# The output product of a hybrid decoder block: eight products of quarters or seven

## The chip, the cores and the metric

The kernel runs on one core of a Trainium2 chip. The core has five engines that run side by side, each with its own queue of instructions: TensorE (PE; its weight loads are shown as PEld), VectorE (DVE), ScalarE (ACT), GpSimd (POOL) and SyncE (SP), which here only starts transfers. The metric is the device time of one execution in microseconds (us), the median of several runs.

## The reference, cut to what matters

The model is one pre-norm decoder layer: 512 tokens, width 1024. Three branches read the normalized input; their gated sum goes through `w_o`, is added to `x`, and a gated convolutional feed-forward block and a last norm follow.

```
u      = rmsnorm(x, ln1_g)
proj   = u @ w_in                      # q, k, v, pool, z, xbc, dt, gates
merged = g0 * (attention @ w_a) + g1 * (pooling @ w_b) + g2 * (ssd @ w_c)
x      = x + merged @ w_o              # the output product: 512 x 1024 by 1024 x 1024
u2     = rmsnorm(x, ln2_g)
x      = x + conv_ffn(u2 @ w_up, ...) @ w_down
out    = rmsnorm(x, final_g)
```

All is float32. TensorE multiplies in fp32r, so every product is made from three: high part by high part, high by low, low by high, where the high part is the value cast to fp32r and the low part what the cast left over (`mm3`, L228).

## The kernel before, in words

**Jobs.** The work is a list of jobs (`program`, L1491). Each job multiplies one piece of weights, usually 128 x 2048 elements: 1 MB that SP loads into `raw` (two buffers), ACT casts to the high part `wh` (two casts of half the columns, L195), and DVE subtracts to the low part `wl` (L215). The loop at L1715 runs the list: as job n begins, `prepare` (L1723) writes the low part of job n+1, then the cast of job n+2, then starts the load of job n+3; then the job's own matmuls are written. A job may have a `form`, a function that makes its weights just ahead of the cast, and a `then`, called behind its low part. With `late` the job's body calls `prepare` itself.

**Order.** PE, ACT, DVE and POOL have their order written out: the program's order is the queue's order (`ORDERED`, L1748). SP's transfers are placed by the scheduler. Work beside the matmuls is in generators: `step()` (L155) moves every generator in `running` on by one yield; `after(n, it)` (L163) holds one back for n steps. So a step is the clock by which side work is laid between matmuls.

**w_c, the third branch.** `branch_jobs(2, w_c, ..., last=True)` (L1219) makes the eight 128-feature pieces m = 0 to 7 of the merged branches, two per job, 24 matmuls of 512 columns each. Its `evac` multiplies by the gate (L1226), adds to the sum `MG[m]` of the other branches (L1227) and splits the result into `MH[m]`, high and low (L1230, L1231). There is one step per piece.

**w_o, the output product.** `load_x1` (L1242) loads the norm's weights and eight 128 x 512 blocks of `x`, `X1[tb, h]`: row block tb (128 tokens), column half h. `wo_jobs(pair, h)` (L1249) computes two row blocks (pair 0: tb 0 and 1; pair 1: tb 2 and 3) of one column half in two jobs of 24 matmuls, four of the eight k slices in each: eight jobs in all, with one step per job. `evac` adds the PSUM bank to `X1` (L1252). After the left half, `norm_early` (L457) squares it on ACT, makes `v0` on DVE and `xg`, x times the norm's weight, on POOL (L462). After the right half, `norm_late` (L466) squares it on ACT, takes the root (L471), multiplies by the weight (L473), makes the factor with three small DVE instructions (L488 to L490) and scales both halves (L492). `norm_turn` (L447) then transposes the block on PE (L451), ACT copies the high part (L454) and DVE makes the low part (L455): `uh` and `ul`, the feed-forward's input. For pair 0 the transposes are held back by one step, for pair 1 they go into the opening of the up projection.

**The opening** (`opening`, L1410): the first two up jobs (up0, up1) multiply tokens 0 to 255 first (L1421), with the transposes of blocks 2 and 3 laid between; the rest of the up projection follows as ordinary matmuls "pu" at L236.

**Seven products.** Elsewhere the kernel already multiplies by quarters with seven products for eight: `Seven` (L344) for parts of w_in and `down_group` (L1349). `sums_of` (L321) makes the sums and differences of a pair of feature pieces: four half additions (L326 to L329), two casts, two low parts (L335, L336). `Seven` makes one weight sum by an adding transfer: `plus` (L354), four POOL transfers of 128 x 512 that add memory to a tile (L356); other weight sums are DVE's (`total`, L358). Tiles "w3" come from a pool of three buffers (`ypool`), shared with the state-space branch.

Of the kernel before, what the change touches and what calls it, by code (L numbers as in the profile page):

```python
# [10 lines left out]
F32 = mybir.dt.float32  # L11
F32R = mybir.dt.float32r
AF = mybir.ActivationFunctionType
OP = mybir.AluOpType
# [68 lines left out]
def trunk(ctx: ExitStack, tc, out, x, rel_bias, ln1_g, w_in, b_gate, w_a, pool_w, pool_scale, w_b,  # L83
# [22 lines left out]
    def T(name, dt=F32, shape=(P, S)):  # L106
        return big.tile(list(shape), dt, name=name, tag="t")
# [55 lines left out]
    def after(n, it):  # L163
        for _ in range(n):
            yield
        yield from it
# [58 lines left out]
    def wsrc(w, k0, k1, c0, c1):  # L225
        return w[k0 * P:k1 * P, c0:c1].rearrange("(k p) c -> p k c", p=P)
# [239 lines left out]
    def norm_late(t, g, v0, outs, last=None):  # L466
# [4 lines left out]
        act.activation(sq, ss, AF.Sqrt, bias=v0, scale=1.0 / D)  # L471
        xg = T("xg")
        dve.tensor_tensor(xg, t, g[1], OP.mult)  # L473
        if last:
            dve.scalar_tensor_tensor(v, ss, -0.5 / D, last, OP.mult, OP.add)
            yield xg

            dve.reciprocal(r, sq)
            dve.scalar_tensor_tensor(rt, r, v, r, OP.mult, OP.mult)
            dve.scalar_tensor_tensor(rt, rt, 1.5, r, OP.add, OP.mult)  # L480

            (o1, x1), (o0, x0) = outs(xg)
            act.mul(o0, x0, rt)
            dve.tensor_scalar(o1, x1, rt, None, OP.mult)
            return
        dve.scalar_tensor_tensor(v, ss, 1.0 / D, v0, OP.mult, OP.add)
        yield xg
        dve.reciprocal(r, sq)  # L488
        dve.scalar_tensor_tensor(rt, r, v, r, OP.mult, OP.mult)
        dve.tensor_scalar(rt, rt, -0.5, 1.5, OP.mult, OP.add)  # L490
        for o, src in outs(xg):
            dve.tensor_scalar(o, src, r, rt, OP.mult, OP.mult)  # L492

    V0 = []

# [708 lines left out]
                    dve.tensor_sub(YT[q][1], Y[gi][:, q % 4, :], YT[q][0].bitcast(F32))  # L1204


    MG, MH, SG = {}, {}, {}

    def gate_jobs(b, lo=0, hi=8):
        def evac(m, ps):  # L1210
# [5 lines left out]

        return jobs_a(w_in, C_GATE + b * D + lo * P, hi - lo, uhk, ulk, KD, evac)

    def branch_jobs(b, w, parts, nk, last=False, more=()):  # L1219
        def evac(m, ps):  # L1220
            if b == 1:
                MG[m] = T("yo")
                act.copy(MG[m], ps)
                return
            s = SG[b, m]
            dve.tensor_tensor(s, s, ps, OP.mult)  # L1226
            (dve if last else pool).tensor_tensor(MG[m], MG[m], s, OP.add)  # L1227
            if last:
                h, l = T("mgh", F32R), T("mgl", F32R)
                act.copy(h, MG[m])  # L1230
                dve.tensor_sub(l, MG[m], h.bitcast(F32))  # L1231
                MH[m] = (h, l)
# [8 lines left out]

    def load_x1():  # L1242
        nxt["g2"] = grow(ln2_g[0])
        for tb in range(4):
            for h in range(2):
                t = X1[tb, h] = T("x1")
                sp.dma_start(t, x[tb * P:(tb + 1) * P, h * S:(h + 1) * S])

    def wo_jobs(pair, h):  # L1249
        def evac(tb, ps):  # L1250
            t = X1[tb, h]
            dve.tensor_tensor(t, t, ps, OP.add)  # L1252
            if h == 0:
                nxt[tb] = norm_early(t, nxt["g2"])
                return
# [3 lines left out]
            v0, xg0 = nxt[tb]  # L1259
            us = [T("u0"), T("u1")]  # L1260
            it = norm_late(t, nxt["g2"], v0, lambda xg1: ((us[0], xg0), (us[1], xg1)))
# [20 lines left out]
        return jobs_b(lambda k0, k1: [wsrc(w_o, k0, k1, h * S, h * S + S)], S,  # L1282
                      lambda k, tb: MH[k][0][:, tb * P:(tb + 1) * P],
                      lambda k, tb: MH[k][1][:, tb * P:(tb + 1) * P], KD, evac,
                      blocks=(2 * pair, 2 * pair + 1), turn_over=pair == 1 and h == 1)


    ACTS = {}
    ff = {}
# [177 lines left out]
    def down_jobs(h):  # L1467

        def evac(tb, ps):
            t = X1[tb, h]  # L1470
            dve.tensor_tensor(t, t, ps, OP.add)
            if h == 0:
                running.append(early(tb))
                return
            v0, vh, xg0 = fin[tb]
            for _ in norm_late(t, fin["g"], v0, lambda xg1: ((xg1, xg1), (xg0, xg0)), last=vh):
# [14 lines left out]
    def program():  # L1491
# [49 lines left out]
        yield from branch_jobs(2, w_c, YT, 8, last=True)  # L1541
        yield Call(load_x1)
        for pair in range(2):
            for h in range(2):
                yield from wo_jobs(pair, h)
            if pair == 0:
# [237 lines left out]
```

## Time and profile before

| | |
|---|---|
| median of three runs | 1021.44 us (1021.38 to 1021.48) |
| the profiled execution: its time | 1021.86 us |
| its span, first to last instruction | 1019.9 us |
| PE busy | 1010.3 us (99%) |
| DVE busy | 707.4 us (69%) |
| ACT busy | 511.3 us (50%) |
| POOL busy | 136.4 us (13%) |
| granted PE clock | 0.998 |

In the rows of the profile, the first number of a timeline row is its start in us from the span's start, the second its length; then the engine, the line of the kernel, the operation, the tiles it writes and reads, their shape, and how many instructions are in the row. In square brackets stands how long the engine was idle before it, and behind the arrow what ended that. Tiles go by the program's names: `pb` are the banks of the output product, `pa` those of w_c and others, `pu` the up projection, `uT` the transposes, `raw`, `wh`, `wl` the weights, `mgh` and `mgl` the merged branches, `w` (for "w3") a weight sum.

### The profile page before, as it was taken

What the parts mean: (1) busy time and instruction counts of PE and PEld (TensorE: products, weight loads), DVE (VectorE), ACT (ScalarE), POOL (GpSimd) and SP (SyncE); (2) the same over time, 40 slices, a digit from 0 to 9 for tenths busy, and PEclk for the clock granted to TensorE, in tenths of its full rate; (3) what the DMA queues carried; (4) which work ended last, traced back from release to release, by engine and by line L of the source; (5) the groups of instructions that cost most, each with busy time, mean ns of one, the idle gap of its engine ahead of it and who ended that gap; (6) DMA issues with size and microseconds to landing.
All of it is one profiled execution on the core that took longest, in us unless ns stands there. A gap on an engine that the chain in (4) does not pass through costs nothing.

```text
span 1019.9 us, 13619 instructions
## 1 busy us (share of the span) xinstructions
PE 1010.3 (99%) x5402; PEld 862.2 (85%) x5402; DVE 707.4 (69%) x886; ACT 511.3 (50%) x863; POOL 136.4 (13%) x120
## 2 busy tenths in 40 slices
PE   8999999999999999999999999999999999999997
PEld 8998878999988888888888888898888888888885
DVE  6564768577767647666889665768778768685756
ACT  5433546564435476879467224554444444433434
POOL 1691000010000000000052501102111100111002
PEclk9999999999999999999999999999999999999999
DMA  8548222255254344552253427532332322321332
GB/s 270 170 101 210 92 74 76 58 149 162 91 183 113 91 124 104 145 141 87 81 155 127 165 85 272 163 124 83 105 102 83 106 101 83 123 83 42 124 103 82
DMA packets 115629, 123.34 MB, mean 121 GB/s; under 512 B 6483, under 2 KB 96150, under 8 KB 115567
## 3 DMA queue, kind: packets, MB, share of 16 engines
q1 hardware_dynamic: 113247, 119.01, 37.5%
q0 software_dynamic: 1728, 2.62, 1.5%
q8 instruction: 42, 0.69, 0.3%
q10 hardware_dynamic: 592, 0.86, 0.2%
q14 instruction: 20, 0.16, 0.0%
HBM read 118.68 MB, written 3.00 MB: 119 GB/s over the span
## 4 chain that ended last, share of the span: by engine, by line
PE 98%; DMA 1%; DVE 0%; ACT 0%; ACTq 0%; issue 0%
PE pa L236 36%; PE pu L236 22%; PE pb L236 12%; PE pd L236 7%; PE pqk L236 6%; PE pq L236 3%; PE pa L1632 2%; PE ps L786 1%; PE pu L1421 1%; PE ppw L236 1%; PE po L834 1%; PE pt L820 1%; PE py L1119 1%; DMA xin<-in_x_dram 1%; PE pyo L1126 1%; PE pst L1107 0%
## 5 line engine op out<-in xcount | busy, mean ns | idle before, releaser
L215 DVE TENSOR_TENSOR wl<-raw,wh 128x2048 fp32r<-128x2048 f32 (+3 forms) x92 | 214.1, 2328 | 51.5 <-ACT wh L195 38.8
L195 ACT CAST wh<-raw 128x1024 fp32r<-128x1024 f32 (+4 forms) x181 | 181.4, 1021 | 57.4 <-DVE raw L359 17.8
L1316 DVE SCALAR_TENSOR_TENSOR hc<-pu,fcol,hc 128x510 f32<-128x510 f32 x88 | 65.9, 748 | 56.2 <-ACT hc L1313 54.5
L236 PE MATMUL pa<-uh,wh 128*128 128x512 f32 (+1 forms) x368 | 88.8, 381 | 0.0
L236 PE MATMUL pa<-ul,wh 128*128 128x512 f32 (+1 forms) x368 | 86.8, 375 | 0.0
L236 PE MATMUL pa<-uh,wl 128*128 128x512 f32 (+1 forms) x368 | 86.8, 375 | 0.0
L236 PE MATMUL pu<-uh,wh 128*128 128x512 f32 (+1 forms) x352 | 83.5, 379 | 0.0
L236 PE MATMUL pu<-ul,wh 128*128 128x512 f32 (+1 forms) x352 | 83.5, 379 | 0.0
L236 PE MATMUL pu<-uh,wl 128*128 128x512 f32 (+1 forms) x352 | 83.5, 379 | 0.0
L236 PEld LDWEIGHTS pa<-ul,wh 128*128 128x128 f32 x368 | 66.7, 188 | 12.6
L236 PEld LDWEIGHTS pa<-uh,wl 128*128 128x128 f32 x368 | 66.7, 188 | 12.5
L236 PEld LDWEIGHTS pa<-uh,wh 128*128 128x128 f32 x368 | 65.4, 189 | 11.8
L236 PEld LDWEIGHTS pu<-ul,wh 128*128 128x128 f32 x352 | 64.2, 188 | 12.5
L236 PEld LDWEIGHTS pu<-uh,wl 128*128 128x128 f32 x352 | 64.2, 188 | 12.5
L236 PEld LDWEIGHTS pu<-uh,wh 128*128 128x128 f32 x352 | 64.1, 188 | 12.4
L1313 ACT ACTIVATE hc<-pu,fcol,fcol 128x512 f32<-128x512 f32 x40 | 31.2, 779 | 78.9 <-PE pu L236 78.9
L1321 POOL TENSOR_TENSOR hc<-hc 128x512 f32<-128x512 f32 x22 | 30.8, 1400 | 289.1 <-DVE hc L1316 244.4
L808 ACT ACTIVATE sb<-sb,nmls 128x128 f32<-128x128 f32 (+1 forms) x72 | 30.0, 418 | 31.4 <-DVE nmls L805 20.8
L215 DVE TENSOR_TENSOR wl<-w,wh 128x2048 fp32r<-128x2048 f32 (+1 forms) x18 | 38.0, 2111 | 10.2 <-issue 4.6
L1102 POOL TENSOR_TENSOR st<-st,dts 128x512 f32<-128x512 f32 x4 | 4.2, 1052 | 225.6 <-ACT st L1110 163.5
L195 ACT CAST wh<-w 128x1024 fp32r<-128x1024 f32 (+1 forms) x36 | 32.9, 954 | 2.4 <-DVE w L341 2.4
L1318 ACT ACTIVATE hc<-hc 128x512 f32<-128x512 f32 x22 | 13.9, 633 | 40.2 <-DVE hc L1316 40.2
(409 smaller groups left out, 1924.4 us busy)
## 6 DMA issues: line engine op xcount, KB each, us to landing
raw<-in_w_in_dram SPq DMA_DIRECT2D x24, 1024.0 KB, 5.8
raw<-in_ffn_w_up_dram SPq DMA_DIRECT2D x22, 1024.0 KB, 5.7
raw<-in_w_o_dram SPq DMA_DIRECT2D x8, 1024.0 KB, 5.1
raw<-in_ffn_w_down_dram SPq DMA_DIRECT2D x8, 1024.0 KB, 5.3
raw<-in_w_in_dram SPq DMA_DIRECT2D x14, 512.0 KB, 5.5
raw<-in_w_in_dram SPq DMA_DIRECT2D x8, 768.0 KB
raw<-in_w_b_dram SPq DMA_DIRECT2D x4, 1024.0 KB
w<-in_ffn_w_down_dram SPq DMA_DIRECT2D x4, 1024.0 KB, 5.0
```

Of the source, the lines that this page charges most:

```text
L195: (other.tensor_copy if other and i else act.copy)(job.high[:, :, o], job.raw[:, :, o])
L215: (eng or dve).tensor_tensor(l[:, :, o], job.raw[:, :, o], h[:, :, o].bitcast(F32), OP.subtract)
L236: pe.matmul(ps, l, r, start=first and n == 0, stop=last and n == total - 1, skip_group_check=onto)
L786: pe.matmul(pss[i][:, o:o + w * P], q[r, n * P:(n + 1) * P], k[r, kb * P:(kb + w) * P], start=True, stop=True)
L808: act.activation(sb[:, off:off + w * P], sb[:, off:off + w * P], AF.Exp, bias=nm[:, n, h:h + 1], accum_out=ls[:, n, h:h + 1])
L820: pe.transpose(pt[:, o:o + P], sb[:, o:o + P], eye)
L834: pe.matmul(po[DH * hh:DH * hh + DH, n * P:(n + 1) * P], V[g, kb + i][:, (2 * c + hh) * DH:(2 * c + hh + 1) * DH], probs[2 * c + hh, nb][: ...
L1313: act.activation(t, ps, AF.Identity, bias=ff["c1"][:, ff["b"] + m:ff["b"] + m + 1], scale=fw(2, m))
L1316: dve.scalar_tensor_tensor(t[:, sh:], ps[:, :S - sh], fw(k, m), t[:, sh:], OP.mult, OP.add)
L1318: act.activation(t, t, AF.Silu)
L1321: pool.tensor_tensor(a, a, t, OP.mult)
L1632: pe.matmul(first[2 * n + j][:, lo:hi], a[:, k, j * P:(j + 1) * P], b[:, k, lo:hi], start=a is wh and b is uh and k == 0, stop=a is wl and ...
```

## The change

The output product becomes one group of seven products of quarters. With the merged branches split by even and odd feature pieces and by token halves, and `w_o` by even and odd k slices and column halves, each of the seven jobs multiplies four k slices by 512 columns for two row blocks: 24 matmuls. Their order is two, five, three, one, six, seven, four.

- The job "two" needs the odd pieces' first token half, "four" the second, "one" the even pieces' first half; "five", "six", "seven" and "three" need the sums 1, 2, 3, 4 of `sums_of`. `merged(m)` makes these while w_c runs. For m = 4 and 5 the addition into `MG[m]` is an adding transfer, and `merged` starts a step later.
- Weights: W0 and W1 are loaded when w_c begins; W0 gets an adding transfer of another quarter at once (`plus(0, 0, 0)`), W1 a second one behind the low part of "three" (`three.then`); W2 = W0 + W1 on DVE, ahead of W1's addition, in w_c's third job. "five" uses W0, "three" the first W1, "six" W2, "seven" the second W1; "four" adds W2 to its raw weights (`total`, on DVE, ahead of its cast). Only "two", "one" and "four" load raw weights.
- Results: "two", "five" and "three" are copied from PSUM to `X1` by ACT, and `x` is added by a transfer, two each, six of the eight blocks. "one", "six", "seven" and "four" are added to or subtracted from `X1` by DVE.
- Bodies step after each row block's bank. "two" and "five" (`apart`) multiply three k slices of both row blocks, step, and then do the fourth.
- The norm: blocks 0 and 1 have their early half behind "one" and their late half behind "six", blocks 2 and 3 behind "seven" (right half first) and "four". The late form scales the late half with one DVE instruction (`apart` in `norm_late`) and the early half on ACT; the form with two DVE scalings goes.

The diff, cut to its core:

```diff
-    def norm_early(t, g):
+    def norm_early(t, g, h=0):
...
-        pool.tensor_tensor(xg, t, g[0], OP.mult)
+        pool.tensor_tensor(xg, t, g[h], OP.mult)
...
+    def norm_late(t, g, v0, outs, last, h=1, apart=False):
         ss, v, sq, r, rt = (small(n, [P, 1]) for n in ("ss", "v", "sq", "r", "rt"))
         squares(act, t, ss)
         act.activation(sq, ss, AF.Sqrt, bias=v0, scale=1.0 / D)
...
+        dve.scalar_tensor_tensor(v, ss, -0.5 / D, last, OP.mult, OP.add)
         yield xg
+
         dve.reciprocal(r, sq)
         dve.scalar_tensor_tensor(rt, r, v, r, OP.mult, OP.mult)
+        dve.scalar_tensor_tensor(rt, rt, 1.5, r, OP.add, OP.mult)
+
+        if apart:
+            o1, (o0, x0) = outs()
+            dve.scalar_tensor_tensor(o1, t, rt, g[h], OP.mult, OP.mult)
+            act.mul(o0, x0, rt)
+            return
...
+    def merged(m):
+        if m % 2 == 0:
+            t = T("m0", F32R)
+            act.copy(t[:, :256], MG[m][:, LO])
+            dve.tensor_sub(t[:, 256:], MG[m][:, LO], t[:, :256].bitcast(F32))
+            MH[m] = (t[:, :256], t[:, 256:])
+            return
+        h, l = T("mgh", F32R), T("mgl", F32R)
+        act.copy(h, MG[m])
+        it = sums_of(MG[m - 1], MG[m], T("sah", F32R), T("sal", F32R),
+                     lambda j, h, l: MS.__setitem__((j, m // 2), (h, l)), True)
+        next(it)
+        dve.tensor_sub(l, MG[m], h.bitcast(F32))
+        MH[m] = (h, l)
+        yield
+        yield from it
...
-            (dve if last else pool).tensor_tensor(MG[m], MG[m], s, OP.add)
+            if last and m in (4, 5):
+                pool.dma_start(MG[m], s, accum_op=OP.add)
+            else:
+                (dve if last else pool).tensor_tensor(MG[m], MG[m], s, OP.add)
             if last:
...
+                running.append(after(1, merged(m)) if m in (4, 5) else merged(m))
...
+        def load():
+            for two in (0, 1):
+                W.append(ypool.tile([P, 4, S], F32, name="w3", tag="xs"))
+                sp.dma_start(W[-1], quarter(two, 1))
+            plus(0, 0, 0)
+
+        def plus(i, two, h):
+            for k in range(4):
+                pool.dma_start(W[i][:, k, :], quarter(two, h)[:, k, :], accum_op=OP.add)
+
+        def sums():
+            W.append(ypool.tile([P, 4, S], F32, name="w3", tag="xs"))
+            dve.tensor_tensor(W[2], W[0], W[1], OP.add)
+
+        def first(tb, h):
+            half = 1 - h
+            v0, xg = norm_early(X1[tb, half], nxt["g2"], half)
+            vh = cpool.tile([P, 1], F32, name=f"vo{tb}")
+            dve.tensor_scalar(vh, v0, -0.5, None, OP.mult)
+            nxt[tb] = v0, vh, xg
+
+        def then(tb, h):
...
+            it = norm_late(X1[tb, h], nxt["g2"], v0,
+                           lambda: (us[h], (us[1 - h], xg0)), vh, h, True)
             next(it)
 
             def rest():
                 next(it, None)
                 yield
                 norm_turn(us, nxt["uh"], nxt["ul"], tb)
 
-            if pair == 0:
+            if tb < 2:
                 r = rest()
                 next(r)
                 running.append(after(1, r))
...
+                def read(i):
+                    tb = 2 * hi + i
+                    if behind is None:
+                        t = X1[tb, h] = T("x1")
+                        act.copy(t, bank[i])
+                        pool.dma_start(t, x[tb * P:(tb + 1) * P, h * S:(h + 1) * S],
+                                       accum_op=OP.add)
+                        return
+                    t = X1[tb, h]
+                    dve.tensor_tensor(t, t, bank[i], op)
+                    behind(tb, h)
+
+                if apart:
+                    for i in range(2):
+                        product(i, range(3), True, False)
+                    step()
+                    parts = side(j)
+                    for i in range(2):
+                        product(i, (3,), False, True)
+                        read(i)
+                    step()
+                    return
+                for i in range(2):
+                    product(i, range(4), True, True)
+                    read(i)
+                    step()
...
+        two = job("A12", quarter(1, 0), None, B, (0, 0), apart=True)
+        five = job(1, None, lambda: W[0], B, (1, 1), apart=True)
+        three = job(4, None, lambda: W[1], B, (0, 1), more=True)
+        one = job("A11", quarter(0, 0), None, A, (0, 0), behind=lambda tb, h: first(tb, 1))
+        six = job(2, None, lambda: W[2], A, (0, 1), more=True, op=OP.subtract, behind=then)
+        seven = job(3, None, lambda: W[1], A, (1, 1), more=True, op=OP.subtract,
+                    behind=lambda tb, h: first(tb, 0))
+        four = job("A22", quarter(1, 0), lambda: total(four.raw, four.raw, W[2]), A, (1, 0), more=True,
+                   behind=then)
+        three.then = lambda: plus(1, 0, 1)
...
+        load, sums, group = wo_group()
+        for i, job in enumerate(branch_jobs(2, w_c, YT, 8, last=True)):
+            if i == 0:
+                yield Call(load)
+            if i == 2:
+                yield Call(sums)
+            if i == 3:
+                yield Call(load_x1)
+            yield job
+        for i, job in enumerate(group):
+            yield job
+            if i == 3:
                 yield Call(ff_cols)
```

More of the change, by code (lines that the diff above doesn't have):

```diff
@@ L471, in norm_late @@
         act.activation(sq, ss, AF.Sqrt, bias=v0, scale=1.0 / D)
[L472 to L486, printed above, removed]
+        xg = None
+        if not apart:
+            xg = T("xg")
+            dve.tensor_tensor(xg, t, g[h], OP.mult)
+        dve.scalar_tensor_tensor(v, ss, -0.5 / D, last, OP.mult, OP.add)
         yield xg
@@ L1243, in load_x1, with wo_group, side @@
         nxt["g2"] = grow(ln2_g[0])
[L1244 to L1255, printed above, removed]
+        for tb in (2, 3):
+            t = X1[tb, 0] = T("x1")
+            sp.dma_start(t, x[tb * P:(tb + 1) * P, :S])
+    def wo_group():
+        quarter = lambda two, h: w_o[:, h * S:(h + 1) * S].rearrange(
+            "(k two p) c -> two p k c", two=2, p=P)[two]
+        W, A, B = [], [], []
+        def side(j):
+            if j == "A11":
+                return [MH[2 * p] for p in range(4)]
+            if j in ("A12", "A22"):
+                half = LO if j == "A12" else HI
+                return [[t[:, half] for t in MH[2 * p + 1]] for p in range(4)]
+            return [MS[j, p] for p in range(4)]
+        def load():
[16 more added lines that the diff above has]
+        def then(tb, h):
             if "uh" not in nxt:
@@ L1280, in evac, with job, body, product @@
                     pass
[L1282 to L1285, printed above, removed]
+        def job(j, raw, form, bank, outs, more=False, op=OP.add, behind=None, apart=False):
+            hi, h = outs
+            def body(ws):
+                wh, wl = ws
+                if not more:
+                    bank[:] = [MM("pb") for _ in range(2)]
+                parts = side(j)
+                def product(i, ks, begin, end):
+                    o = slice(i * P, (i + 1) * P)
+                    mm3(bank[i], lambda k: wh[:, k, :], lambda k: wl[:, k, :],
+                        lambda k: parts[k][0][:, o], lambda k: parts[k][1][:, o], ks, begin, end,
+                        flip=True, onto=more)
+                def read(i):
[13 more added lines that the diff above has]
+                    step()
+                    parts = side(j)
+                    for i in range(2):
[7 more added lines that the diff above has]
+                    step()
+            new = Job([raw] if raw is not None else [], 4, S, body)
+            new.form, new.once = form, True
+            if raw is None:
+                new.load = lambda: None
+            return new
@@ new lines, in total @@
+        def total(out, a, b, op=OP.add):
+            dve.tensor_tensor(out, a, b, op)
+            return out
+        two = job("A12", quarter(1, 0), None, B, (0, 0), apart=True)
[3 more added lines that the diff above has]
+        six = job(2, None, lambda: W[2], A, (0, 1), more=True, op=OP.subtract, behind=then)
@@ new lines, in wo_group, with body @@
+        seven = job(3, None, lambda: W[1], A, (1, 1), more=True, op=OP.subtract,
[3 more added lines that the diff above has]
+        three.then = lambda: plus(1, 0, 1)
+        four.late, inner = True, four.body
+        def body(ws):
+            late_split.append(four.prepare(later=True))
+            inner(ws)
+        four.body = body
+        return load, sums, [two, five, three, one, six, seven, four]
@@ L1475, in evac @@
             v0, vh, xg0 = fin[tb]
-            for _ in norm_late(t, fin["g"], v0, lambda xg1: ((xg1, xg1), (xg0, xg0)), last=vh):
+            for _ in norm_late(t, fin["g"], v0, lambda xg1: ((xg1, xg1), (xg0, xg0)), vh):
                 xg1 = _
```

22 lines of the change are left out of this document (5 added, 17 removed).

## The prediction

> **What bounds the kernel now.** I read the page first (busy shares, chain of work that ended last), then the chain in order of time, then each engine's instructions around the output product.
>
> ```profile
> PE 1010.3 (99%) x5402; PEld 862.2 (85%) x5402; DVE 707.4 (69%) x886; ACT 511.3 (50%) x863; POOL 136.4 (13%) x120
> PE 98%; DMA 1%; DVE 0%; ACT 0%; ACTq 0%; issue 0%
> 534.39 81.63 PE pa L236 x360
> 616.02 27.20 PE pb L236 x120
> 643.23 1.75 PE uT L451 x16
> 644.97 10.91 PE pb L236 x48
> 656.19 5.64 PE pb L236 x24
> 661.83 3.83 PE pu L1421 x32
> 665.66 0.87 PE uT L451 x8
> 672.50 0.87 PE uT L451 x8
> 673.37 1.91 PE pu L1421 x16
> 675.28 98.59 PE pu L236 x480
> 773.86 5.44 PE pd L236 x24
> ```
>
> TensorE (PE) is the bound: it holds 98% of the chain. The output product is the 192 matmuls "pb" from 616.02 to 661.83, two groups of transposes inside it. 24 matmuls take 5.44 us wherever nothing waits (last row). So a matmul taken away is worth 0.227 us, but only while VectorE (DVE), ScalarE (ACT) and the transfers keep ahead of PE. I count T in us from 615.9, where the product's first matmul starts; in T its transposes stand at 27.3, the up projection opens at 45.9 and its ordinary matmuls begin at 59.4 (675.28).
>
> **What goes.** Seven products of 24 matmuls stand for eight: 24 fewer, 5.44 us. One weight split goes (one DVE low part, two ACT casts) and, per row block, a DVE product and a second scaling. Input: five raw loads fewer, two W loads and the transfers below in their place.
>
> **What comes, and whether DVE and ACT stay ahead.** The rows that give the durations:
>
> ```profile
> 616.06 0.69 DVE L1226 TENSOR_TENSOR sg<-sg,pa 128x512 f32<-128x512 f32 x1 [2.58 <-PE pa L236]
> 616.85 0.69 DVE L1227 TENSOR_TENSOR yo<-yo,sg 128x512 f32<-128x512 f32 x1
> 628.29 3.88 ACT L195 CAST wh<-raw 128x1024 fp32r<-128x1024 f32 x4
> 630.31 4.49 DVE L215 TENSOR_TENSOR wl<-raw,wh 128x2048 fp32r<-128x2048 f32 x2 [1.73 <-ACT wh L195]
> 635.10 0.69 DVE L1252 TENSOR_TENSOR x<-x,pb 128x512 f32<-128x512 f32 x1 [0.30 <-PE pb L236]
> 635.82 0.63 ACT L437 ACTIVATE junk<-x 128x512 f32<-128x512 f32 x1 [3.65 <-DVE x L1252]
> 636.57 1.28 ACT L471 ACT_TABLE_LOAD   x1
> 637.86 0.29 ACT L471 ACTIVATE sq<-ss,v 128x1 f32<-128x1 f32 x1
> 638.19 0.16 DVE L488 RECIPROCAL r<-sq 128x1 f32<-128x1 f32 x1 [1.45 <-ACT sq L471]
> 638.90 1.00 DVE L492 TENSOR_SCALAR u<-xg,r,rt 128x512 f32<-128x512 f32 x2
> 643.07 1.91 PE L451 MATMUL uT<-eye,u 128*128 128x128 f32 x16
> 695.62 0.41 DVE L326 TENSOR_TENSOR sa<-hc 128x256 f32<-128x256 f32 x1
> 696.74 0.42 DVE L329 TENSOR_TENSOR sb<-hc,sa 128x256 f32<-128x256 f32 x1
> L335 DVE TENSOR_TENSOR sal<-sa,sah x12: 679/681/693, 100.2 to 885.0; 128x512 fp32r<-128x512 f32 x12
> L359 DVE TENSOR_TENSOR w<-w,w x3: 1757/1758/2292, 183.3 to 254.9; 128x1536 f32<-128x1536 f32 x2, 128x2048 f32<-128x2048 f32 x1
> L483 ACT ACTIVATE xg<-xg,rt x4: 722/724/725, 1004.8 to 1015.8; 128x512 f32<-128x512 f32 x4
> ```
>
> DVE, ACT and POOL run in program order: the two low parts at 630.31, written ahead of the evacuation at 635.10, also ran ahead of it. So I lay the new program on these queues.
>
> *Sums of the merged branches, w_c's last two pieces.* Per pair: four half sums (1.54 us, 695.62 to the end of 696.74), two casts, two low parts of 0.68. Under w_c they lie in DVE's waits (2.58 us ahead of 616.06): free. The last pair doesn't: evacuation T 0.2, add 1.0, sums 1.8 to 3.3, low part of piece 7 to 3.9, just under the 4.08 us that 18 matmuls of the split first product ("two") cover. Then low(five), 2.25, to 6.1 and the low part of pair 2's sums to 6.8. PE wants that one five matmuls into "five", its weights 0.2 ahead: 6.35. Wait **0.45 us**; bounds 0 and 1.5 (if the adding transfer of MG[5] lands late).
>
> *Adding transfers.* Sixteen in all (8 for weights, 2 for MG, 6 for x), each 128 rows of 2 KB, issued by POOL. What the trace shows of them:
>
> ```profile
> 72.94 2.84 POOL L356 DMA_DIRECT2D w<-in_w_in_dram  x3
> 80.50 0.88 POOL L356 DMA_DIRECT2D w<-in_w_in_dram  x1 [4.72 <-issue]
> 221.90 2.65 POOL L356 DMA_DIRECT2D w<-in_w_in_dram  x3 [132.70 <-DVE yo L742]
> 227.52 0.88 POOL L356 DMA_DIRECT2D w<-in_w_in_dram  x1 [2.97 <-issue]
> DMA to landing us min/median/max: 3.6/6.2/9.0
> ```
>
> Three go out back to back and the fourth waits until about the first has landed: 5.6 or 7.6 us from first to fourth. The first weight sum has all of w_c (43 us) as cover, the MG ones 5.4 us each: free. The second, into W1, is issued behind low(three), which by the queue above ends at T 10.8 (6.8 + three low parts of 0.6 + 2.25). Its fourth part goes out at 16.4 to 18.4 and lands 3.6 to 6.2 later, 20.0 to 24.6; I take **21.5**, nearer the group at 221.90, which was as lightly loaded. Behind it wait on ACT: the cast of "seven" (ACT reaches it at 17.5), then the squares of "one"; on DVE the v0 and vh of "one"; behind the same POOL queue four transfers of x and POOL's xg. At two per 5 us these x blocks land by about T 29; the first is wanted at E.
>
> [...]
>
> *The evacuation of "six".* This is the step that costs. Between the last evacuation of "one" and the first of "six" the program puts on DVE low(seven) and the sum four.raw + W2 (L359's 2048 form, 2.29; together 4.5, as the two at 630.31), and on ACT the two casts of "four", ahead of the square of row block 0. With the cast of "seven" done at C = 21.5 + 1.95 = 23.45: square of block 0, v0, vh, evacuation of block 1, its square, v0, vh: C + 2.95 (0.72 from evacuation to square, 0.75 per square, 0.4 for the two small ones). Then the 4.5: the evacuation of "six" starts at **E = C + 7.45 = 30.9**. Its bank was full at T 24.9. If the transfer costs nothing, "one"'s second bank sets the start (22.4) and E is 28.75: the floor.
>
> From E: ACT casts "four" until E + 1.95, squares to 2.75, loads the root's table and takes the root (1.28 + 0.29) to 4.35, DVE's three small ones 0.71 (638.19 to 638.90) to 5.05, ACT scales the early half (L483, 0.72) to 5.8. There the transposes can start: T 36.7. Now the place: before, the transposes of blocks 0 and 1 stood one job (5.44 us) behind their evacuation; now after(1, r) is counted in half jobs, since job bodies step after each bank, so block 0's transposes stand right behind "six"'s second bank, at T 27.2 + 0.45 = 27.7. **PE waits 9.0 us** (7.0 at the floor). Even a DVE that was free at once would leave 24.9 + 4.6 - 27.7 = 1.8 us.
>
> *After that.* DVE stays behind PE: from E, block 0 and 1 to 9.0, low parts of block 0's u to 10.9, low(four) to 13.1, evacuations and norms of "seven" and block 1's u to 18.7, those of "four" to 22.6, low(up0) to 25.8, hardly a gap between them. PE, released at E + 5.8, does transposes, "seven", "four" and the first 32 matmuls of the up projection and its transposes by E + 23.4, then wants low(up0): **2.4 us** more. The ordinary matmuls begin at E + 34.4 = T 65.3, against 59.4.
>
> **The sum.** 65.3 - 59.4 = +5.9 us; as waits: -5.44 + 0.45 + 9.0 + 2.4, less 0.5 us of small waits that before has there. POOL's xg can also fall on a DVE instruction:
>
> ```profile
> 711.12 1.33 POOL L1321 TENSOR_TENSOR hc<-hc 128x512 f32<-128x512 f32 x1 [3.81 <-DVE hc L1316]
> 711.22 3.38 DVE L215 TENSOR_TENSOR wl<-raw,wh 128x2048 fp32r<-128x2048 f32 x1
> ```
>
> There a low part took 3.38 for 2.25: up to 1.1 us for each of two such meetings ahead of E; I take 0.1. So +6.0. Behind T 65 PE is the bound as before and gives nothing back. The profiled execution took 1021.86 (span 1019.9 and 2.0 around it), 0.4 over the median of 1021.44; on the median I forecast **1027.4 us**. Floor 1021.44 + 3.75 = 1025.2, and 1.3 less if the table is already loaded: 1024.0. Top: landing 24.6 (+3.1) and an xg meeting (+1.1): 1031.5.
>
> **Rivals.**
> 1. *DVE is not late* (not slower). If low(seven) and the sum ran ahead of "one"'s evacuations, where DVE idles 3 us, it would take "six"'s bank when it is full, E = 24.9, and ACT's square would come at once, 1.2 us sooner against E. Then PE waits 1.8 at the transposes, and the DVE chain behind E still sets the opening: E + 33.2 = 58.1, -1.3 us, 1020.1. It ends on the other side from E = 26.2 on downwards. If besides the transposes stand later in PE's order than I read, so that PE waits nowhere: -5.44, 1016.0. For it: DVE's idle time, and that before reaches these transposes without a wait (643.07). Against: program order, seen at 630.31. Chances 0.08 for the first, 0.12 for the second.
> 2. *PE's clock falls in the 9 us of idleness.*
>
> ```profile
> 1.06 5.29 PE L1591 MATMUL pa<-ones 128*128 128x128 f32 x24 [1.06 <-DVE ones L1582]
> 6.75 2.05 PE L1649 MATMUL uT<-diag,xin 128*128 128x128 f32 x16 [0.41 <-DVE diag L1661]
> PE uT L1649 <- DVE diag L1661: 1.7, 2, 1.3
> ```
>
> The first matmuls after idleness took 0.22 us each, later ones of the same shape 0.13. [...] Chance 0.14. [...] PE's longest wait in this trace is 1.3 us (last row), so no row tests it.
> 3. *The x transfers set E.* If each takes the longest time shown, 9.0, with three in flight, those of "three" land at T 34 instead of 29: E 34, +3.1, 1030.5; they decide once they land behind E. Chance 0.08.
>
> That fewer matmuls aren't made is excluded: 7 x 24 are written.
>
> **Chances.** Forecast 0.58, rival 1 0.08 and 0.12, rival 2 0.14, rival 3 0.08. The range 1024.0 to 1031.5 holds the forecast, rival 2 and most of 3. 0.2% (2.0 us) is about what a measurement here can tell from no change. Faster (1016.0) 0.12, same (1020.1) 0.08, slower 0.80.
>
> **What would show it.** The chain of waits after: PE "uT" behind an ACT u, once, some 9 us, between "six" and "seven"; PE behind DVE's wl 2.4 us at the opening; ACT's cast of w3 behind a DMA for 3 to 6 us; "pb" with 168 matmuls; DVE low(seven) and the total ahead of the evacuation of "six". Wrong if the transposes stand later in PE's order, if DVE reaches "six"'s bank by T 25, or if the fourth part of W1's sum lands before T 17.5 (then 1025).

## The result and the profile after

The changed kernel takes 1035.39 us (median of four runs, 1034.82 to 1036.01), the kernel before, timed beside it, 1021.41 us: a ratio of 1.0137 (95% interval 1.0120 to 1.0155), 14.0 us slower. The forecast was 1027.4 with a range up to 1031.5. The direction was right, the size was not.

The page of the changed kernel, busy time and chain of work that ended last:

```profile
span 1033.1 us, 13637 instructions
PE 1010.9 (98%) x5378; PEld 861.1 (83%) x5378; DVE 714.3 (69%) x905; ACT 519.7 (50%) x879; POOL 147.9 (14%) x136
PE 93%; DVE 2%; DMA 2%; ACT 1%; issue 1%; POOL 0%; ACTq 0%; DVEq 0%; POOLq 0%
```

PE makes 24 matmuls fewer and is yet no less busy: some of them ran slower (mean granted clock 0.990, against 0.998 before). And 5% of the chain that PE held has gone to DVE, transfers, ACT and issue. The view of PE's waits in this stretch (waiting engine, tile and line, what ended it, then us in total, times, longest) says where:

```profile
PE uT L451 <- ACT u L486: 7.5, 1, 7.5
PE pb L236 <- DVE x L1350: 3.1, 1, 3.1
PE pb L236 <- DVE mgl L1229: 2.0, 1, 2.0
```

The timeline of PE gives their places and the end of the opening:

```profile
618.78 0.50 PE L236 MATMUL pb<-wh,mgl 128*128 128x512 f32 x1 [2.00 <-DVE mgl L1229]
647.46 2.08 PE L236 MATMUL pb<-wh,sah 128*128 128x512 f32 x4 [3.06 <-DVE x L1350]
659.44 1.97 PE L451 MATMUL uT<-eye,u 128*128 128x128 f32 x8 [7.53 <-ACT u L486]
688.13 1.12 PE L236 MATMUL pu<-uh,wh 128*128 128x256 f32 x8
```

The product's first matmul starts at 615.49 here, so the waits stand at T 3.3 ("two"), 32.0 (second half of "six") and 44.0 (the transposes), and the ordinary up matmuls begin at T 72.6, against 59.4 before: 13.2 us, which is all that the span grew by. Everything was lost in the stretch that the prediction worked out.

What ACT was waiting for, from its waits (yo<-sg are the two transfers into MG, w<-in_w_o_dram is W1's second sum):

```profile
ACT m L1220 <- DMA yo<-sg: 12.5, 1, 12.5
ACT wh L195 <- DMA w<-in_w_o_dram: 6.9, 1, 6.9
```

DVE's waits show who stood behind ACT:

```profile
DVE m L1221 <- ACT m L1220: 5.9, 1, 5.9
```

And the view of the line that issues the transfers into MG has their way to landing:

```profile
DMA to landing us min/median/max: 7.8/8.1/8.5
```

The timeline of POOL shows the issues, the two for MG and the four of W1's second sum:

```profile
604.37 0.86 POOL L1243 DMA_DIRECT2D yo<-sg  x1 [19.97 <-DVE sg L1241]
606.17 0.86 POOL L1243 DMA_DIRECT2D yo<-sg  x1 [0.93 <-DVE sal L335]
...
629.87 0.86 POOL L1285 DMA_DIRECT2D w<-in_w_o_dram  x1 [2.67 <-DVE wl L215]
632.54 0.86 POOL L1285 DMA_DIRECT2D w<-in_w_o_dram  x1 [1.81 <-issue]
633.82 0.89 POOL L1285 DMA_DIRECT2D w<-in_w_o_dram  x1 [0.42 <-issue]
635.16 0.88 POOL L1285 DMA_DIRECT2D w<-in_w_o_dram  x1 [0.45 <-issue]
```

And the chain, in order of time (start, length, what), from that fourth part to the transposes:

```profile
635.16 8.54 DMA w<-in_w_o_dram
643.80 1.99 ACT wh L195 x2
...
646.71 0.70 DVE x L1350
...
651.32 2.29 DVE raw L1375
653.70 1.99 ACT wh L195 x2
...
658.67 0.73 ACT u L486
...
659.44 1.97 PE uT L451 x8
```

This is the prediction's mechanism link by link: the fourth part lands, ACT casts "seven", the norms of "one" follow, DVE does low(seven) and the sum for "four", and only then evacuates the first bank of "six":

```profile
653.52 0.68 DVE L1350 TENSOR_TENSOR x<-x,pb 128x512 f32<-128x512 f32 x1
```

That is E = T 38.0, where 30.9 was forecast. From E on the forecast came out in numbers: transposes at E + 5.9 (forecast 5.8), end of the opening at E + 34.6 (34.4). So 7.1 of the 7.3 us between forecast and trace lie ahead of E. The second of the two numbers is partly luck, as e3 shows below: the forecast had TensorE wait 2.4 us there for low(up0), the low part of up0's weights, but TensorE came to that place late and found it done (the row shows no wait):

```profile
679.52 2.15 PE L1530 MATMUL pu<-uh,wl 128*128 128x256 f32 x16
```

### The profile page after: what moved, and what is told of

The parts are those of the page before. It is cut to its first block, busy times and chain, and to the rows that moved or that the text cites. A ratio compares the mean times of both kernels' runs of the same rounds, so it can differ in the third digit from the quotient of the medians.

```text
span 1033.1 us, 13637 instructions
## 1 busy us (share of the span) xinstructions
PE 1010.9 (98%) x5378; PEld 861.1 (83%) x5378; DVE 714.3 (69%) x905; ACT 519.7 (50%) x879; POOL 147.9 (14%) x136
## 4 chain that ended last, share of the span: by engine, by line
PE 93%; DVE 2%; DMA 2%; ACT 1%; issue 1%; POOL 0%; ACTq 0%; DVEq 0%; POOLq 0%
PE pa L236 33%; PE pu L236 22%; PE pb L236 10%; PE pd L236 7%; PE pqk L236 6%; PE pq L236 3%; PE pa L1747 2%; PE ps L784 1%; PE pu L1530 1%; PE ppw L236 1%; PE po L832 1%; DMA w<-in_w_o_dram 1%; PE pt L818 1%; PE py L1117 1%; DMA yo<-sg 1%
## 5 line engine op out<-in xcount | busy, mean ns | idle before, releaser
L215 DVE TENSOR_TENSOR wl<-raw,wh 128x2048 fp32r<-128x2048 f32 (+3 forms) x87 | 202.7, 2330 | 48.1 <-ACT wh L195 34.4
L195 ACT CAST wh<-raw 128x1024 fp32r<-128x1024 f32 (+4 forms) x171 | 171.5, 1020 | 68.6 <-DVE raw L359 17.8
L236 PEld LDWEIGHTS pa<-ul,wh 128*128 128x128 f32 x368 | 66.7, 188 | 12.6
L236 PEld LDWEIGHTS pa<-uh,wl 128*128 128x128 f32 x368 | 66.7, 188 | 12.5
L215 DVE TENSOR_TENSOR wl<-w,wh 128x2048 fp32r<-128x2048 f32 (+1 forms) x22 | 47.7, 2167 | 13.7 <-PE pb L236 4.9
L195 ACT CAST wh<-w 128x1024 fp32r<-128x1024 f32 (+1 forms) x44 | 41.0, 971 | 9.3 <-DMA w<-in_w_o_dram 6.9
```

The source lines that it names most:

```text
L195: (other.tensor_copy if other and i else act.copy)(job.high[:, :, o], job.raw[:, :, o])
L215: (eng or dve).tensor_tensor(l[:, :, o], job.raw[:, :, o], h[:, :, o].bitcast(F32), OP.subtract)
L236: pe.matmul(ps, l, r, start=first and n == 0, stop=last and n == total - 1, skip_group_check=onto)
```

## The experiments

Theory A: the queue that DVE and ACT share from E on sets the end, some 34 us behind E, and E is late because the adding transfers land late. The rivals: the half clock behind PE's waits is the loss; the transfer into W1 doesn't matter; the place of the transposes in PE's order is the loss. In the table T runs from each kernel's own first "pb" matmul; E is the start of the first evacuation of "six", the end is the first ordinary up matmul, both from the timelines. They belong to the one profiled execution of each kernel, whose time differs from the median: by 1.6 us in e1 (1030.93) and 1.4 in e8 (1021.58), by 0.7 or less in the others. The ratios are to the kernel before as timed beside each run, on several chips (1021.37 to 1021.65 for e1 to e12).

| kernel | us, median | ratio to before (95%) | E, T | end, T | end - E |
|---|---|---|---|---|---|
| before | 1021.4 | 1 | | 59.4 | |
| after | 1035.39 | 1.0137 (1.0120 to 1.0155) | 38.0 | 72.6 | 34.6 |
| e1, MG by DVE | 1032.48 | 1.0105 (1.0090 to 1.0120) | 35.4 | 69.1 | 33.8 |
| e2, W1 by DVE | 1030.89 | 1.0090 (1.0075 to 1.0105) | 34.7 | 69.1 | 34.4 |
| e3, wait filled | 1034.24 | 1.0125 (1.0108 to 1.0142) | 38.3 | 71.8 | 33.5 |
| e4, transposes later | 1035.03 | 1.0132 (1.0117 to 1.0147) | 39.0 | 73.4 | 34.4 |
| e5, e1 and e2 | 1027.87 | 1.0058 (1.0043 to 1.0073) | 31.0 | 66.2 | 35.2 |
| e6, and four's sum early | 1024.14 | 1.0023 (1.0014 to 1.0032) | 28.8 | 62.2 | 33.4 |
| e7, all sums early | 1020.54 | 0.9989 (0.9980 to 0.9999) | 25.3 | 58.1 | 32.8 |
| e8, e7 and transposes later | 1020.16 | 0.9986 (0.9976 to 0.9995) | 25.3 | 59.1 | 33.8 |
| e11, e7 and columns early | 1020.96 | 0.9996 (0.9987 to 1.0005) | 26.1 | 58.9 | 32.8 |
| e12, e8 and columns early | 1020.46 | 0.9991 (0.9982 to 1.0000) | 26.5 | 58.8 | 32.3 |

**e1: the two sums into MG by DVE.**

```diff
-            if last and m in (4, 5):
-                pool.dma_start(MG[m], s, accum_op=OP.add)
-            else:
-                (dve if last else pool).tensor_tensor(MG[m], MG[m], s, OP.add)
+            (dve if last else pool).tensor_tensor(MG[m], MG[m], s, OP.add)
```

> Only the additions into MG[4] and MG[5] go back to VectorE; they took 7.8 and 8.5 us as adding transfers, and ScalarE and VectorE stood behind them. Theory A (the queue of VectorE sets the end: the opening is over 34.4 us behind the evacuation of six, and that evacuation hangs on the landing of W1's second sum, which hangs on low(three), 3.4 us late through MG): the evacuation of six comes about 3.4 us earlier, 1031.9 us in all; the 2.0 us wait in two and the half clock behind it are gone too, and that is the same time, not more. Rival B (TensorE's waits and its half clock add up, each by itself): minus 2.0 and minus 1.9 for that place, and what W1 lands earlier on top, 1028.

2.9 us off. PE's waits:

```profile
PE uT L451 <- ACT u L486: 7.8, 1, 7.8
PE pb L236 <- DVE x L1347: 3.9, 1, 3.9
```

The wait in "two" is gone, though two DVE additions came in its place, and W1's second sum starts 3.3 us earlier, at T 11.1 (the forecast had 10.8):

```profile
626.21 0.88 POOL L1282 DMA_DIRECT2D w<-in_w_o_dram  x1 [3.18 <-DVE wl L215]
```

The time is theory A's 1031.9 within 0.6, with E 2.7 us earlier (A had 3.4), and not the 1028 of its rival.

**e2: W1's second sum by DVE.**

```diff
-        seven = job(3, None, lambda: W[1], A, (1, 1), ...
+        seven = job(3, quarter(0, 1), lambda: total(seven.raw, seven.raw, W[1]), A, (1, 1), ...
-        three.then = lambda: plus(1, 0, 1)
```

> Only the second weight sum goes from an adding transfer to VectorE: the weights of seven are loaded as raw and W1 is added ahead of the cast (2.29 us of VectorE more, four adding transfers less). A: the cast of seven waits no longer for the landing at T 28.2 but for VectorE's sum, done about 2.5 us earlier, so the evacuation of six and the end come 2 to 3 us earlier: 1032.5 to 1033.5 us. Rival C (the transfer is not the last thing that seven's cast waits for; VectorE's load is): no better, 1035 to 1037.

4.5 us off: more than theory A expected, and the theory by which it would be no better falls, though DVE has one 2.3 us instruction more and SP a load of 1 MB. The 3.1 us wait in the second half of "six" went as well:

```profile
PE uT L451 <- ACT u L486: 8.5, 1, 8.5
PE pb L236 <- DVE mgl L1229: 2.0, 1, 2.0
```

So that wait had the same cause. "six" adds onto the banks of "one", and its second half can't start until DVE has read the second bank of "one", which stood behind the norm of the first, behind ACT's cast of "seven", behind the transfer.

**e3: the 7.5 us wait filled.** 30 matmuls whose result nobody reads stand ahead of block 0's transposes.

```diff
+                if tb == 0:
+                    ps = SM("fill")
+                    for i in range(30):
+                        pe.matmul(ps, ones, MH[7][0], start=i == 0, stop=i == 29)
                 norm_turn(us, nxt["uh"], nxt["ul"], tb)
```

> Thirty matmuls of no use are put into the 7.5 us in which TensorE waits for the transposes of row block 0; the outputs don't use them. Clock: the granted clock behind the wait stays at 1.0 instead of 0.5, and seven's first half takes 2.7 us instead of 4.3. A: the end does not move by it, because low(up0) on VectorE is wanted just when it is there: 1035 us, within 0.5 us. Rival B (the half clock is on the path): minus 2.3 us, 1033.

1.15 us off, between the 1035 of A and the 1033 of the half clock. With PE at full clock behind the wait, the wait for low(up0) that the prediction had listed shows itself:

```profile
678.70 2.17 PE L1534 MATMUL pu<-uh,wl 128*128 128x256 f32 x16 [0.29 <-DVE wl L215]
```

So the half clock behind this wait is worth about 1.1 us of the end (end - E 33.5 in place of 34.6); then DVE's queue is the bound again. In time that is little more than the scatter of four runs (1033.22 to 1034.94 here, 1034.82 to 1036.01 before the edit).

**e4: the transposes one half job later.**

```diff
-                running.append(after(1, r))
+                running.append(after(2, r))
```

> Only the place of the transposes of row blocks 0 and 1 in TensorE's order changes: one half job later. The recorded prediction named that place as what lets TensorE wait. A: TensorE's wait gets shorter and moves, the end stays, since the queue of VectorE sets it: 1034.5 to 1035.5 us. Rival D (the place is the loss): up to 4 us less, 1031.

0.4 us off, within A's range and far from the 1031 of the rival. PE's waits only move: the one ahead of the transposes is 3.5 us, and PE waits 7.0 in two pieces for banks, where it had waited 3.1 in one. All its waits together are 13.0 us, against 12.6.

```profile
PE pb L236 <- DVE x L1350: 7.0, 2, 4.0
PE uT L451 <- DVE fcol L517: 3.5, 1, 3.5
```

**e5: e1 and e2 together.**

> MG[4], MG[5] and W1's second sum are all added by DVE; only W1's first sum and the six additions of x are still left to adding transfers or to what the changed kernel does with them. Theory A (the landing of the two kinds of transfer sets when DVE reaches the evacuation of the second half of six, and the end of the opening follows 33.5 to 34.6 us behind that): DVE would reach it at about 646 us against 653.5, the opening would end at about 680, and the time is about 1026 us, below both e1 (1032.5) and e2 (1030.9); the two gains of 2.9 and 4.5 us add up, since they are two separate delays of one queue. Rival F (the two transfers share one cause, so that undoing one already took most of the other): 1029 to 1031.

1027.87 lies between A's 1026 and the rival's 1029 to 1031, and by the time alone it is nearer to the rival. What speaks for A is that the gains add up: E is 7.0 us earlier than in the changed kernel, against 2.7 and 3.3 for the parts, and the time 7.5 us shorter, against 2.9 and 4.5. These are two separate delays of one queue. E came where it was expected, at 646.2, the end 1.4 us later than the 680. One wait of PE is left, the 8.5 us ahead of the transposes, and half clock behind it. In the windows of e5 the first two numbers are the window's length and PE's busy time, then come the other engines; the granted clock is the third number from the end:

```profile
652.00:656.00 4.00, 3.91 (x14) 3.43 (x15) 2.40 (x8) 2.62 (x7) 0.00 (x0) 0.50 0.00 0
```

**e6: as e5, and the sum for "four" by DVE between "three" and "one".** Its raw quarter is loaded into the buffer of W0, which is free by then.

```diff
-        four = job("A22", quarter(1, 0), lambda: total(four.raw, four.raw, W[2]), ...
+        four = job("A22", None, lambda: W[3], ...
+            W.append(ypool.tile([P, 4, S], F32, name="w3", tag="xs"))
+            sp.dma_start(W[3], quarter(1, 0))
...
+            total(W[3], W[3], W[2])
```

> As e5, and the sum for the weights of four is made ahead of one, in a buffer that is free by then, so that it and the cast that waits for it leave the stretch ahead of the transposes. Theory A: DVE reaches the second half of six at about 644 us, the chain behind it is 1.2 us shorter, time about 1023 us. Rival (the order of DVE no longer decides, the PE stream at half clock does): no gain on e5.

1024.14, 3.7 below e5 where A had 3, with E at 644.0 as expected; the rival's "no gain" falls. No adding transfer was touched: one 2.3 us sum was moved to a place where DVE has time, and the load of its raw quarter with it.

**e7: the sum for "seven" early too, and "six" with `late`.** Low(seven) and the cast of "four" are written behind the first evacuation of "six", beside the norm; the root's table is loaded ahead by an activation of no use.

```diff
-        seven = job(3, quarter(0, 1), lambda: total(seven.raw, seven.raw, W[1]), ...
+        seven = job(3, quarter(0, 1), None, ...
+        six.late = True
+        held_back.append(lambda: six.prepare())
...
+            total(seven.raw, seven.raw, W[1])
             total(W[3], W[3], W[2])
+            act.activation(small("pre", [P, 1]), eps, AF.Sqrt)
...
             if tb < 2:
+                if held_back:
+                    held_back.pop()()
                 r = rest()
```

> No adding transfer for MG and for W1's second sum, the sums for seven and four both made between three and one, and the low part for seven and the cast for four written behind the first half of six, beside the norm, whose table is loaded ahead by an activation of no use. Theory A: DVE evacuates the second half of six as soon as its bank is full; what is left is some 3 us of DVE work too much between six and the first ordinary up job. Time 1018.7 to 1020 us, so faster than before (1021.4). If the 7 products cost PE more than their 24 matmuls save, it stays above 1021.4 in spite of that.

1020.54: above theory A's 1018.7 to 1020, and faster than before, barely (0.9989, interval 0.9980 to 0.9999). DVE now waits for the bank of "six" instead of the bank for DVE, as its timeline shows, and PE waits some 3 us in place of 12.6:

```profile
641.20 0.69 DVE L1350 TENSOR_TENSOR x<-x,pb 128x512 f32<-128x512 f32 x1 [0.90 <-PE pb L236]
```

```profile
PE uT L451 <- ACT u L486: 2.6, 1, 2.6
PE pu L1541 <- DVE wl L215: 0.3, 1, 0.3
PE uT L451 <- DVE ul L455: 0.2, 1, 0.2
```

**e8: e7 with the transposes of e4.**

> As e7, with the transposes of blocks 0 and 1 one half job later in PE's order. Theory A: in e7 PE waits about 2 us for block 0 and runs at half clock behind it; here that wait is covered, 1018 us or less. Rival: DVE is late by over 2.7 us there, so PE waits for a bank of its accumulators instead, and the time is that of e7.

1020.16 (0.9986, interval 0.9976 to 0.9995): as e7. The wait for block 0 is gone, and one of the same length stands ahead of block 1's transposes, for the evacuation of the convolution's columns. The expectation of 1018 or less missed; its rival, that DVE's lateness only shows elsewhere, held, though the wait is not for a bank of the accumulators, as it had said.

```profile
653.74 1.21 PE L451 MATMUL uT<-eye,u 128*128 128x128 f32 x8 [2.53 <-DVE fcol L517]
```

**e9 and e10: transfers by themselves.** e5 with three transfers of 256 KB into buffers that nobody reads any more: alone, beside the loads that the changed kernel has at that place (here a load of 1 MB more, which starts at 609.7 in e5 and not at 615.3), and alone from memory. In e9 they add, in e10 they don't. Each is one execution.

```diff
+            if last and m == 3:
+                pool.dma_start(s, MG[m], accum_op=OP.add)
+            if last and m == 5:
+                pool.dma_start(s, MG[m], accum_op=OP.add)
+            if last and m == 7:
+                pool.dma_start(s, x[0:P, 0:S], accum_op=OP.add)
```

> e5 with three adding transfers of 256 KB whose results nobody reads: behind piece 3 of w_c (about 595, no other transfer under way) and behind piece 5 (about 605, beside the same loads of weights, gain rows and x as the changed kernel's) from buffer to buffer, behind piece 7 (about 616, alone) from memory to buffer. Theory T1 (the landing of 7.8 to 8.5 us is contention with the other loads): about 4 us for the first, 7 to 8.5 for the second, about 4 for the third. Theory T2 (an adding transfer from buffer to buffer is slow by itself): 7 to 8 us for the first two, less for the third. The time itself is not looked at.

> e9 with plain transfers on the same queue, places and sizes in the place of the adding ones, so that what is left of a difference is the price of adding. T1: within 0.5 us of e9's three. T2: 2 to 4 us less for the first two.

The times from issue to landing in the views of the three lines, e9 and then e10:

```profile
DMA to landing us min/median/max: 3.3/3.3/3.3
DMA to landing us min/median/max: 6.2/6.2/6.2
DMA to landing us min/median/max: 4.1/4.1/4.1
```

```profile
DMA to landing us min/median/max: 2.3/2.3/2.3
DMA to landing us min/median/max: 5.9/5.9/5.9
DMA to landing us min/median/max: 2.9/2.9/2.9
```

T2 falls: from buffer to buffer an adding transfer takes 3.3 us alone. T1 holds in kind: the other loads cost it 2.9 us (and the plain one 3.6), though its 7 to 8.5 for the second was too high, and so was its view of adding: that costs 1.0 and 1.2 us alone, 0.3 beside other loads. In e9's windows, the last two columns (busy share of the DMA engines, GB/s) tell the two places apart. The column of DVE, 3.97 of 4.00 us at the first place, shows that a busy DVE doesn't by itself make the landing long:

```profile
596.00:600.00 4.00, 4.00 (x19) 3.30 (x19) 3.97 (x7) 2.86 (x4) 0.55 (x1) 1.00 0.38 66
606.00:612.00 6.00, 6.00 (x28) 4.97 (x27) 5.58 (x8) 1.12 (x3) 0.86 (x1) 1.00 1.06 321
```

In the changed kernel two of them were under way together there, and took 7.8 and 8.5; that the second one makes the difference to 6.2 was not tested.

**e11 and e12: the columns' load, transposes and evacuations three jobs earlier** in e7 and in e8.

```diff
-            if i == 3:
+            if i == 0:
                 yield Call(ff_cols)
```

> e7 with the load, transposes and evacuations of the convolution's columns three jobs earlier, ahead of one, so that they leave DVE's full queue between six and the up projection. Theory A (that queue sets the end): 0.5 to 0.8 us off, 1019.9. If the 2.6 us wait ahead of the transposes sets it, no change: 1020.5.

> e8 with the same move. In e8 PE waits 2.5 us for the columns' evacuation ahead of block 1's transposes, at half clock behind it. Theory A: DVE is full there, so the wait goes only as far as DVE's queue gets shorter and stays as a wait for a bank: 0.5 to 1 us off, 1019.4. If the wait is due to the columns alone, 2.5 to 4 us off: 1016.5 to 1017.7.

Neither differs from its base by what these runs can tell (1020.96 and 1020.46), so A, which had 1019.9 and 1019.4, missed both. e11 keeps e7's wait (2.5 us here), and its alternative, no change, held. In e12 the 2.5 us wait is gone, but not the time, as it would be (1016.5 to 1017.7) were the columns alone its cause; two others stand for it:

```profile
PE pu L1541 <- DVE wl L215: 1.7, 1, 1.7
PE pb L236 <- DVE x L1350: 1.2, 1, 1.2
```

Four orders of the same work (e7, e8, e11, e12) end at T 58.1 to 59.1. PE's waits move among them, and the end stays 32.3 to 33.8 us behind E. In e11 and e12 E itself comes 0.8 and 1.2 us later than in e7 and e8, while the end stays as far behind E as before in e11 (32.8 us) and comes 1.5 us closer to it in e12: what the move may gain behind E is lost ahead of it.

## Why the prediction was wrong, step by step

The chain that the forecast described is the one that ran. What failed are two of its terms, both of them the time that adding transfers take to land.

- *24 matmuls, -5.44.* They are gone, but even in e7 only 1.3 us of it reaches the end. Rival 1 had just this: E at 24.9, the end at E + 33.2 = T 58.1, -1.3 us, 1020.1. e7 measured E 25.3, end 58.1, 1020.54. So that rival's price came out, in part by luck: e7 also loads the root's table ahead and casts "four" behind E, which the rival's sum doesn't have, and its low(seven) stands behind E, where the rival had it ahead of "one". To make DVE punctual took all these edits: two kinds of sums off the transfers, two sums made earlier, and the low part, the cast and the table moved.
- *Adding transfers: "the MG ones 5.4 us each: free".* **This step failed.** They took 7.8 and 8.5 us. Behind them ACT stood 12.5 us and DVE 5.9; pieces 6 and 7 of w_c were evacuated late, PE waited 2.0 in "two" (0.45 in "five" was forecast, 1.5 the upper bound), and W1's second sum was issued at T 14.4 instead of 10.8. e1 undid this: first issue at T 11.1, 2.9 us back.
- *W1's second sum lands at T 21.5, at most 24.6.* **This failed too.** It landed at T 28.2. Of the 6.7 us, 3.6 are the late start just told, the rest the way from first issue to last landing, 13.8 us where 10.7 was taken. The term of that sum that was too small is the landing: the fourth part went out 5.3 us behind the first, not later than the forecast's 5.6 to 7.6, and landed 8.5 us after that. In e1, where the start is as forecast, it still took 14.3 (626.21 to the cast at 640.6). The bound took 3.6 to 6.2 from a row that reads 3.6/6.2/9.0: the third number, which these parts came close to (8.5 here), was used for x in rival 3 and left out here. And the stretch was taken to be "as lightly loaded" as the one at 221.90, while x's own transfers and SP's loads keep the DMA engines full (1.00 over 15 us, the second number from the end; from 220 on, the three 4 us windows of the kernel before read 0.53, 1.10 and 0.48):

```profile
629.00:644.00 15.00, 15.00 (x66) 12.07 (x65) 5.73 (x4) 4.45 (x7) 5.21 (x6) 1.00 1.00 215
```

- *E = C + 7.45.* Held: the cast of "seven" ended at T 30.3, E came 7.7 later. low(seven) took 2.83 us beside POOL's xg, not 2.25: one of the meetings that the prediction had named.
- *E + 5.8, E + 34.4.* Within 0.2. The first held by its mechanism, the second in part by luck. The 2.4 us wait for low(up0) in it didn't come, and PE's half clock behind the transposes took its place; with full clock (e3) PE waits 0.3 us for low(up0), 0.9 us sooner behind E than the forecast's E + 25.8, and the end is at E + 33.5. Through all kernels of the table end - E stayed between 32.3 and 35.2. With both transfers undone (e5), E is 31.0 and the time 1027.87: the forecast's 30.9 and 1027.4. That is no proof of its transfer times, since in e5 DVE carries the sums instead.
- *PE waits 9.0 at the transposes, 2.4 for low(up0).* 7.5 and none: PE came later to both places, by the waits in "two" and "six" and by its half clock. The wait in "six" (3.1) wasn't in the sum; as far as e2 shows, it changed nothing in the end: without it the end came 3.5 us earlier, as E did (3.3).
- *Rival 2, the clock.* The rows that the rival goes by show no fall: from 0 to 9 us of the kernel before, with its matmuls of 0.22 us, the granted clock reads 1.00. In the changed kernel it fell to 0.50, and not only with the long wait that the rival named: behind the waits of 2.0 and 3.1 us as well as 7.5. As waits the loss reads: -5.4 and -0.5 for the small waits of before, + 12.6, which leaves some 6.5 of the 13.2 us. In windows of 1 us the clock is at half for 3.4, 3.1 and 4.8 us of matmuls behind the three waits; half of that, 5.6 us, is an estimate of what it cost PE. But e3, which lifts the half clock behind the third wait alone, shows only 1.1 us of it in the end, so it was mostly hidden.
- *Rival 3, x sets E.* No wait on an x transfer in the trace; the chain runs through W1's.

## What to carry to other kernels

An adding transfer of 256 KB took 3.3 us alone, 6.2 beside other loads, 7.8 and 8.5 in the changed kernel. It is not free because it has cover: price it by what else the DMA engines carry at that place and by the longest landing in the profile, and then ask which engine waits behind it in order. When fewer matmuls meet a vector engine that is already late, lay its queue out first; here the order of two 2.3 us sums, a low part, a cast and a table load (e5 to e7) was worth 7.3 us, more than the 5.4 of the products saved. Where four orders of the same work end within 1 us of each other, as here, don't expect much more from reordering of that kind.

## What the runs showed of the hardware

The granted clock fell to half behind waits of 2.0 and 3.1 us, not only behind 7.5. The windows behind these three in the changed kernel:

```profile
620.00:622.00 2.00, 2.00 (x6) 1.54 (x6) 1.93 (x6) 1.45 (x2) 0.00 (x0) 0.50 0.00 0
647.50:650.00 2.50, 2.50 (x6) 2.02 (x7) 1.75 (x3) 0.66 (x2) 1.73 (x2) 0.50 0.79 120
659.50:663.00 3.50, 3.50 (x13) 3.12 (x14) 1.91 (x6) 2.24 (x6) 0.00 (x0) 0.50 0.00 0
```

But a wait of 2.55 us gave half clock in e11 and full clock in e7, with the same PE program up to there but for the columns' two transposes:

```profile
647.30:649.00 1.70, 1.68 (x9) 1.68 (x10) 0.74 (x3) 1.02 (x3) 0.00 (x0) 0.61 0.95 290
```

```profile
646.40:648.00 1.60, 1.56 (x11) 1.48 (x12) 0.71 (x2) 0.99 (x3) 0.00 (x0) 1.00 0.85 275
```

The 0.61 of e11 is full clock for some 0.4 us and half clock from there on (0.50 from 649 to 651 us). So at this length the fall isn't settled by the wait alone. Nor does the half clock always last the same: by the means of windows of 0.5 and 1 us it lasts 3.4 us for the 2.0 us wait of the changed kernel (619.85 to 623.26) and for the 3.1 us one (647.16 to 650.57), and 10.2 us for the 7.5 us one: it begins inside the wait (0.99 from 653 to 654, 0.50 from 654 on) and ends at 664.2, 4.8 us behind it (0.89 from 664 to 665). What sets its begin and its length no run here tests.
